# A two-layer hybrid decoder on one core: gate and up of two feature blocks by seven half-width products in place of eight

## The chip, the core and the metric

The kernel runs on one core of one Trainium2 chip. The metric is the device time of one execution in microseconds. Everything is float32; each float32 operand of a matrix product is held as two parts, a rounded "hi" part and the remainder "lo", both of type fp32r.

## The reference, cut to what matters

Two layers, each with a feed-forward network (FFN), a mixer (attention, a state-space scan and gates) and a second FFN. The change touches the FFN alone:

```python
D_MODEL, SEQ, DEPTH, FFN_HIDDEN = 1024, 512, 2, 2816

def swiglu(h, w_up, w_down):
    gate, up = jnp.split(h @ w_up, 2, axis=-1)
    return (jax.nn.silu(gate) * up) @ w_down

for l in range(DEPTH):
    x = x + 0.5 * swiglu(rms_norm(x, ffn1_norm[l]), ffn1_w_up[l], ffn1_w_down[l])
    ...                                   # the mixer
    x = x + 0.5 * swiglu(rms_norm(x, ffn2_norm[l]), ffn2_w_up[l], ffn2_w_down[l])
```

## The kernel before, in words

Activations lie transposed: 8 tiles `x` of 128 features by 512 tokens. All weights come from one flat array, in units of 128 output features; a unit of 1024 input features is 128 x 1024 in SBUF (8 blocks of 128 x 128, 512 KB). `unit_order` lists the units in the order in which TensorE (PE) uses them, and everything else follows this list.

For each unit three steps run ahead of PE. `fetch` has SyncE (SP) issue the load into `wraw` (3 buffers). `convert` has ScalarE (ACT) round it to `whi` and VectorE (DVE) subtract, which gives `wlo` (3 buffers of each). `ahead` starts the conversion of the unit two places ahead (`LOOK`) and fetches up to four ahead (`AHEAD`). PE then multiplies with `dense`: for each of the 8 blocks `mm3` makes three matmuls, whi by hi, wlo by hi and whi by lo, with the weight block as the stationary operand and 512 tokens as the moving one. A unit of 8 blocks is 24 matmuls of 512 columns into one PSUM bank.

Side work (conversions, activations, norms) is written as generators. `tick` runs one step of each after every block of `dense`, so each engine's program is one fixed order that the generators and ticks decide. Engines run their programs in order and wait for one another by semaphores.

In the FFN the 22 feature blocks of 128 go in slices of 8, 8 and 6. In a slice each block has a gate unit and an up unit; ACT takes Silu of the gate out of PSUM (`g`), DVE multiplies by up (`a`), ACT and DVE split the result (`act`, hi and lo). Then eight down units of 8 or 6 blocks consume the slice's `act` and DVE adds them to `x`. At the start of an FFN the norm's scale is not ready, so the first blocks use unnormed `h`, and DVE scales the 8 tiles `tt`; from then on `h` is the normed pair.

Of the kernel before, what the change touches and what calls it, by code (L numbers as in the profile page):

```python
# [7 lines left out]
F32 = mybir.dt.float32  # L8
# [3 lines left out]
ALU = mybir.AluOpType  # L12
# [19 lines left out]
FB = FFN // P  # L32
SLICES = ((0, 8), (8, 16), (16, 22))
EPS = 1e-6
KCONV = 4
# [48 lines left out]


def unit_order(layer):

    def ffn(f):
        for s, (j0, j1) in enumerate(SLICES):
            for j in range(j0, j1):  # L90
                yield (layer, f, "gate", j), KB
                yield (layer, f, "up", j), KB
            for m in range(KB):
                yield (layer, f, "down", s, m), j1 - j0
# [24 lines left out]
def all_units():  # L119
    table, off = {}, 0  # L120
    for layer in range(DEPTH):
        for key, n in unit_order(layer):
            table[key] = (off, n)
            off += n * P * P
    return table, off


class Builder:
# [8 lines left out]
    def __init__(self, ctx, tc, xT, wflat, par, taps, out):  # L137
        self.tc, self.nc = tc, tc.nc
        self.ctx = ctx
        self.xT, self.wflat, self.par, self.taps, self.out = xT, wflat, par, taps, out  # L140
        self.units, _ = all_units()
        self.keys = list(self.units)
        self.pos = 0
        self.raw, self.loaded = [], []
        self.count = 0
        self.side = []
        self.xd = None

    def name(self, s):
# [33 lines left out]


    def fetch(self, i):
        off, n = self.units[self.keys[i]]
        raw = self.t(self.wraw, [P, KB * P], "wraw")
        self.nc.sync.dma_start(raw[:, :n * P], self.wflat[off:off + n * P * P].rearrange("(p f) -> p f", p=P))
        self.raw.append(raw)

    def convert(self, i):
# [52 lines left out]
    def project(self, *key, swap=False, aside=False):  # L244
# [5 lines left out]
        if swap and not normed and self.scaled_blocks >= KB // 2:  # L250
            new = []
            each = self.swapped(new)
            for _ in range(len(self.hx)):
                next(each)
            self.dense(ps, w, self.h, 0, KB, each=each)
            self.h, self.normed = new, True
        else:
            self.dense(ps, w, self.h, 0, KB)
# [11 lines left out]
    def scale_blocks(self, gain):  # L270
# [3 lines left out]
        for k in range(KB):  # L274
            self.nc.vector.scalar_tensor_tensor(self.tt[k], self.x[k], gain[:, k:k + 1], self.rs,  # L275
                                                op0=ALU.mult, op1=ALU.mult)
            self.scaled_blocks = k + 1
            yield 1

    def open_norm(self, tiles, gain):  # L280
# [166 lines left out]

    def up(self, pu, g, fp, ap, act):
        while not self.gated.pop(g.name, False):
# [3 lines left out]
        yield 1  # L453
        parts = self.pair(ap, ("act", "act"))
        yield from self.split(parts, a)
        act.append(parts)

# [6 lines left out]
    def x_final(self, m, gain):  # L464
# [4 lines left out]
        else:  # L469
            self.xg.append(self.t(self.fin, [P, SEQ], "xg", bufs=KB))  # L470
        if m == 0:
# [9 lines left out]
    def ffn(self, layer, f, gain, gain_next):  # L481
        tc = self.tc
        with tc.tile_pool(name=f"act{layer}{f}", bufs=18, reuse_waits="tile") as ap, \
                tc.tile_pool(name=f"ffn{layer}{f}", bufs=3, reuse_waits="tile") as fp, \
                tc.tile_pool(name=f"hx{layer}{f}", bufs=self.SPARE, reuse_waits="tile") as hx, \
                tc.tile_pool(name=f"tt{layer}{f}", bufs=KB, reuse_waits="tile") as tp:
            self.hx = [self.pair(hx, ("xhi", "xlo")) for _ in range(self.SPARE)]
            self.gated = {}
            self.open_norm([self.t(tp, [P, SEQ], "tt") for _ in range(KB)], gain)
            for s, (j0, j1) in enumerate(SLICES):  # L490
                act = []
                last = s == len(SLICES) - 1
                for j in range(j0, j1):
                    g = self.t(fp, [P, SEQ], "g")
# [7 lines left out]
                    self.spawn(self.up(pu, g, fp, ap, act))  # L502
                for m in range(KB):
# [405 lines left out]
    def mixer(self, layer):  # L909
# [3 lines left out]
        self.open_norm(self.x, gain)  # L913
        self.hx = []
        first = []
# [95 lines left out]
    def build(self):  # L1011
# [24 lines left out]
        for layer in range(DEPTH):  # L1036
# [3 lines left out]
            if layer < DEPTH - 1:  # L1040
                self.ffn(layer, 2, par[:, G_FFN2:G_FFN2 + KB], self.pars[layer + 1][:, G_FFN1:G_FFN1 + KB])
        with tc.tile_pool(name="fin", bufs=KB, reuse_waits="tile") as self.fin:
            self.xg = []
            self.ffn(DEPTH - 1, 2, self.pars[DEPTH - 1][:, G_FFN2:G_FFN2 + KB], None)
            self.flush()
            for m in range(KB):
                nc.vector.tensor_tensor(self.xg[m], self.xg[m], self.rs, op=ALU.mult)
                nc.sync.dma_start(self.out[m], self.xg[m])
        self.xpool.__exit__(None, None, None)
# [8 lines left out]
def lay_out(inputs):  # L1058
# [6 lines left out]
    for layer in range(DEPTH):  # L1065
# [5 lines left out]
        for key, n in unit_order(layer):  # L1071
            kind = key[1] if key[1] not in (1, 2) else key[2]
            if kind in ("gate", "up"):
                w = a[f"ffn{key[1]}_w_up"][layer]
# [76 lines left out]
```

## Time and profile before

| | |
|---|---|
| median of 3 runs | 2695.17 us (2694.84 to 2695.27) |
| the profiled execution, its own time | 2694.19 us |
| its span (first to last instruction) | 2692.4 us |
| PE busy | 2661.0 us, 99% of the span |
| DVE, ACT, GpSimd (POOL) busy | 1363.8, 1103.5, 329.6 us |
| granted TensorE clock | 0.997 of full |

The stretches 987.90 to 1076.30 and 1119.80 to 1206.90 are gate and up of the first and second slice of layer 0's second FFN. In the timelines below a row is the start in us from the span's start, the duration in us, engine, line, operation, what is written and read, the shape and the count; square brackets hold the engine's idle time ahead of it and what ended it. PEld is the loading of a stationary operand, which runs beside the matmuls. A matmul's end is modelled; starts are recorded. Rows with a count are several instructions merged, so a duration there is from the first start to the last end.

### The profile page before, as it was taken

The numbers are of one execution on the slowest core, as the hardware profiler recorded it, in microseconds if no ns is written. First come the engines' busy times: TensorE is split into PE (matmuls) and PEld (weight loads), VectorE is DVE, ScalarE is ACT, GpSimd is POOL, SyncE is SP. The second block draws the span as 40 slices with busy tenths as digits, with TensorE's granted clock in tenths as the row PEclk, the third lists the DMA queues.
The fourth block names the chain that finished last, engine by engine and source line by source line (L and its number), as shares of the span: only waits on it lengthen the run. The fifth ranks groups of instructions, "written<-read, shape, count | busy, mean of one in ns | idle before, by whom it ended". The sixth has DMA issues, their size and how long they took to land.

```text
span 2692.4 us, 31240 instructions
## 1 busy us (share of the span) xinstructions
PE 2661.0 (99%) x12264; PEld 2211.6 (82%) x12264; DVE 1363.8 (51%) x1943; ACT 1103.5 (41%) x1835; POOL 329.6 (12%) x475
## 2 busy tenths in 40 slices
PE   8999999999999999999999999999999999999998
PEld 6888888888888888888888888888888888888886
DVE  6333366565665464333563333765666745733333
ACT  5222246755554243222332222567555543422223
POOL 1000011042332010000010000112332410100001
PEclk9999999999999999999999999999999999999999
DMA  3332242233323423223233222423333243232322
GB/s 131 101 97 94 95 124 82 90 111 105 114 94 116 143 91 110 94 94 102 87 101 102 94 96 90 132 70 106 104 112 109 94 135 124 95 101 94 102 92 73
DMA packets 85828, 276.15 MB, mean 103 GB/s; under 512 B 10112, under 2 KB 10368, under 8 KB 85680
## 3 DMA queue, kind: packets, MB, share of 16 engines
q1 hardware_dynamic: 84816, 273.03, 31.2%
q8 instruction: 96, 1.57, 0.2%
q10 hardware_dynamic: 864, 1.12, 0.1%
q14 instruction: 52, 0.43, 0.1%
HBM read 261.43 MB, written 12.68 MB: 102 GB/s over the span
## 4 chain that ended last, share of the span: by engine, by line
PE 90%; DVE 6%; ACT 2%; issue 1%; DMA 0%; POOL 0%; SPq 0%; DVEq 0%; ACTq 0%
PE mm L227 28%; PE mm L229 28%; PE mm L228 27%; PE pt L577 1%; PE pa L812 1%; DVE wlo L201 1%; PE pa L650 1%; ACT whi L199 1%; DVE cv L714 1%; DVE tt L275 1%; PE pa L814 1%; PE pt L797 1%; PE pt L795 1%; DVE hlo L385 0%; PE pt L411 0%
## 5 line engine op out<-in xcount | busy, mean ns | idle before, releaser
L227 PE MATMUL mm<-hhi,whi 128*128 128x512 f32 x2148 | 859.3, 400 | 0.4 <-DVE g L430 0.4
L229 PE MATMUL mm<-hlo,whi 128*128 128x512 f32 x2148 | 839.7, 391 | 1.3 <-DVE hlo L267 1.3
L228 PE MATMUL mm<-hhi,wlo 128*128 128x512 f32 x2148 | 837.3, 390 | 0.0
L199 ACT CAST whi<-wraw 128x1024 fp32r<-128x1024 f32 (+2 forms) x472 | 473.6, 1003 | 868.3 <-PE mm L229 515.3
L201 DVE TENSOR_TENSOR wlo<-wraw,whi 128x1024 fp32r<-128x1024 f32 (+2 forms) x472 | 585.2, 1241 | 405.9 <-ACT whi L199 404.2
L229 PEld LDWEIGHTS mm<-hlo,whi 128*128 128x128 f32 x2148 | 403.6, 188 | 90.2 <-DVE hlo L267 3.4
L228 PEld LDWEIGHTS mm<-hhi,wlo 128*128 128x128 f32 x2148 | 404.5, 188 | 78.6 <-issue 1.2
L227 PEld LDWEIGHTS mm<-hhi,whi 128*128 128x128 f32 x2148 | 404.4, 188 | 78.3 <-issue 2.0
L229 PE MATMUL mm<-act,whi 128*128 128x512 f32 x704 | 273.9, 389 | 0.0
L227 PE MATMUL mm<-act,whi 128*128 128x512 f32 x704 | 273.9, 389 | 0.0
L228 PE MATMUL mm<-act,wlo 128*128 128x512 f32 x704 | 273.9, 389 | 0.0
L403 POOL TENSOR_TENSOR acc<-acc,sq 128x512 f32<-128x512 f32 x39 | 53.1, 1362 | 1548.7 <-ACT sq L396 1548.7
L460 DVE SCALAR_TENSOR_TENSOR x<-mm,x 128x512 f32<-128x512 f32 x96 | 66.2, 689 | 214.9 <-PE mm L229 214.9
L438 ACT ACTIVATE g<-mm 128x512 f32<-128x512 f32 x79 | 47.3, 598 | 293.0 <-PE mm L229 293.0
L452 DVE TENSOR_TENSOR a<-mm,g 128x512 f32<-128x512 f32 x88 | 60.8, 691 | 207.7 <-PE mm L229 203.0
L714 DVE SCALAR_TENSOR_TENSOR cv<-mm,conv,cv 128x511 f32<-128x511 f32 (+2 forms) x192 | 142.7, 744 | 25.7 <-ACT cv L711 24.0
L227 PEld LDWEIGHTS mm<-act,whi 128*128 128x128 f32 x704 | 132.2, 188 | 27.5
L229 PEld LDWEIGHTS mm<-act,whi 128*128 128x128 f32 x704 | 132.2, 188 | 27.4
L228 PEld LDWEIGHTS mm<-act,wlo 128*128 128x128 f32 x704 | 132.2, 188 | 27.4
L229 PE MATMUL mm<-xlo,whi 128*128 128x512 f32 x316 | 123.0, 389 | 0.0
L228 PE MATMUL mm<-xhi,wlo 128*128 128x512 f32 x316 | 123.0, 389 | 0.0
L227 PE MATMUL mm<-xhi,whi 128*128 128x512 f32 x316 | 122.9, 389 | 0.0
(232 smaller groups left out, 2942.5 us busy)
## 6 DMA issues: line engine op xcount, KB each, us to landing
wraw<-in_wflat_dram SPq DMA_DIRECT2D x392, 512.0 KB, 3.3
wraw<-in_wflat_dram SPq DMA_DIRECT2D x64, 384.0 KB, 3.1
cumb<-cum_d SPq DMA_DIRECT2D x16, 768.0 KB, 4.0
xd<-x SPq DMA_DIRECT2D x16, 256.0 KB, 3.8
wraw<-in_wflat_dram SPq DMA_DIRECT2D x16, 256.0 KB, 2.9
x<-xd SPq DMA_DIRECT2D x16, 256.0 KB, 4.5
gd<-gs SPq DMA_DIRECT2D x12, 256.0 KB, 2.0
gd<-gm SPq DMA_DIRECT2D x12, 256.0 KB, 2.0
```

The costliest lines, as they stand in the source:

```text
L199: nc.scalar.copy(hi[:, :n], raw[:, :n])
L201: nc.vector.tensor_tensor(lo[:, :n], raw[:, :n], hi[:, :n].bitcast(F32), op=ALU.subtract)
L227: mm(ps, a[0], b[0], start=start, stop=False, **kw)
L228: mm(ps, a[1], b[0], start=False, stop=False, **kw)
L229: mm(ps, a[0], b[1], start=False, stop=stop, **kw)
L275: self.nc.vector.scalar_tensor_tensor(self.tt[k], self.x[k], gain[:, k:k + 1], self.rs, op0=ALU.mult, op1=ALU.mult)
L403: eng.tensor_tensor(self.acc, self.acc, sq, op=ALU.add)
L438: nc.scalar.activation(g, pg, AF.Silu)
L452: self.nc.vector.tensor_tensor(a, pu, g, op=ALU.mult)
L460: self.nc.vector.scalar_tensor_tensor(x, pd, 0.5, x, op0=ALU.mult, op1=ALU.add)
L577: self.nc.tensor.transpose(pt[:, cs], src[:, cs], self.ident)
L714: nc.vector.scalar_tensor_tensor(u[:, i:], ps[:, :SEQ - i], tap[KCONV - 1 - i], u[:, i:], op0=ALU.mult, op1=ALU.add)
```

## The change: what it does

Gate and up of two feature blocks j and j+1 are taken together. Cut the input features in a lower and an upper half (4 blocks each) and the tokens in halves a and b (256 columns each). A part then holds half the input features and both feature blocks (8 blocks of 128 x 128, again 512 KB). The parts are named after the seven products: "11" and "12" are the lower and upper half of gate, "22" the upper half of up; the stored part "s1" is the lower half of up. Four are sums: s1 is that lower half plus "22", s3 is it plus "11"; for both the flat array's "s1" part is loaded by SP and the second summand added by a DMA that POOL issues (`accum_op=add`) into the same buffer. s2 = s1 + "11" and s4 = s2 + "12" are made by DVE.

`combine` makes from the normed tiles `tt` the activation differences in place, once in each FFN (16 DVE operations of 256 columns, 8 ACT casts and 8 DVE remainders of 512), as pairs `th`, `tt`.

`pair_of_blocks` runs the products in the order 11, 12, s2, s1, s3, s4, 22. Each is 2 feature blocks x 4 input blocks x 3 = 24 matmuls of 256 columns. One bank ("chain") collects 11, s2, s3 and 22 one after the other and is read between them; "12" goes to a second bank, s1 and s4 to a third. ACT copies out of PSUM (`g1`, `g2`, `c`), DVE adds (`g1`, `c`, `g2`), and `activate` makes Silu, the product with up (negated) and the split, once for each token half.

This is done for all blocks from the fifth on, from the seventh in the first FFN of layer 0 (`pairs_from`): 9 + 9 + 9 + 8 = 35 pairs. The other blocks stay as they were. A unit of a pair ticks after every second block, so four times.

```diff
+SEVEN = ("11", "12", "s2", "s1", "s3", "s4", "22")
+STORED = ("11", "12", "s1", "22")
+def pairs_from(layer, f):
+    return 6 if (layer, f) == (0, 1) else 4
...
+        for i, key in enumerate(self.keys):
+            if "pair" in key and key[-1] in ("s1", "s3"):
+                self.early.setdefault(i - (5 if key[-1] == "s1" else 4), []).append(key)
...
     def fetch(self, i):
...
+        for key in self.early.get(i, ()):
+            base = key[:-1]
+            raw = self.sums[key] = self.t(self.sx, [P, KB * P], key[-1], bufs=2)
+            self.nc.sync.dma_start(raw, self.stored(base + ("s1",)))
+            self.nc.gpsimd.dma_start(raw, self.stored(base + ("22" if key[-1] == "s1" else "11",)), accum_op=ALU.add)
...
     def convert(self, i):
...
+                raw = self.sums[key] = self.t(self.sx, [P, KB * P], "s2", bufs=1)
+                a, b = self.sums[base + ("s1",)], self.sums.pop(base + ("11",))
...
+            nc.vector.tensor_tensor(raw, a, b, op=ALU.add)
+            yield 1
...
+    def combine(self):
...
+            nc.vector.tensor_tensor(u[:, a], u[:, a], u[:, b], op=ALU.subtract)
+            nc.vector.tensor_tensor(u[:, b], v[:, b], u[:, b], op=ALU.subtract)
...
+    def pair_of_blocks(self, base, fp, two):
...
+        def product(ps, part, rhs, cols, start):
+            hi, lo = self.unit(*base, part)
+            for j in range(2):
+                for k in range(n):
+                    ks = slice((j * n + k) * P, (j * n + k + 1) * P)
+                    self.mm3(ps[:, j * half:(j + 1) * half], (hi[:, ks], lo[:, ks]),
+                             [r[:, cols] for r in rhs[k]], start and j + k == 0, k == n - 1, skip_group_check=True)
+                    if k % 2:
+                        self.tick()
...
+        product(chain, "11", lower, a, True)
+        nc.scalar.copy(g1, chain)
+        product(ps2, "12", upper, a, True)
+        nc.vector.tensor_tensor(g1, g1, ps2, op=ALU.add)
+        self.spawn(activate(g1, up1, a))
+        product(chain, "s2", diff[n:], b, False)
+        nc.scalar.copy(g2, chain)
+        product(ps3, "s1", diff[:n], a, True)
+        c = self.t(fp, [P, SEQ], "c", bufs=2)
+        nc.scalar.copy(c, ps3)
+        product(chain, "s3", diff[:n], b, False)
+        nc.vector.tensor_tensor(c, chain, c, op=ALU.add)
+        up2.append(c)
+        product(ps3, "s4", upper, b, False)
+        nc.vector.tensor_tensor(g2, g2, ps3, op=ALU.add)
+        self.spawn(activate(g2, up2, b))
+        product(chain, "22", diff[n:], a, False)
+        up1.append(chain)
```

Where instructions stand now is shown at three places, all in the second FFN of layer 0. L numbers are of the kernel that the rows belong to.

PE before, at the seam from a gate unit (`mm_9311`) to an up unit (`mm_9348`); `xhi`, `hhi` and `hlo` are normed activations:

```order
L227 MATMUL mm_9311<-hhi_8274,whi_9249 128x512
L228 MATMUL mm_9311<-hhi_8274,wlo_9250 128x512
L229 MATMUL mm_9311<-hlo_8275,whi_9249 128x512
L227 MATMUL mm_9348<-xhi_8079,whi_9285 128x512 [waits Activation_49]
L228 MATMUL mm_9348<-xhi_8079,wlo_9286 128x512 [waits DVE_49]
```

PE of the change, at the seam from product "12" (`mm_10245`) to s2, which goes on in the chain bank (`mm_10244`):

```order
L269 MATMUL mm_10245<-hhi_9094,whi_10216 128x256
L270 MATMUL mm_10245<-hhi_9094,wlo_10217 128x256
L271 MATMUL mm_10245<-hlo_9095,whi_10216 128x256
L269 MATMUL mm_10244<-th_8896,whi_10265 128x256 [waits Activation_49]
L270 MATMUL mm_10244<-th_8896,wlo_10266 128x256 [waits DVE_49]
```

The three matmuls of a block stay together and each keeps its own weight load; the columns fall from 512 to 256, and the waits for `whi` (ACT) and `wlo` (DVE) come at each product's first and second matmul.

DVE before, one whole block (a gate and an up unit):

```order
L201 TENSOR_TENSOR wlo_9320<-wraw_9242,whi_9319 128x1024 [waits DMAHW5_49]
L201 TENSOR_TENSOR wlo_9356<-wraw_9279,whi_9355 128x1024 [waits DMAHW6_49,PE_49,Activation_49]
L452 TENSOR_TENSOR a_9387<-mm_9348,g_9310 128x512 [waits PE_49]
L293 TENSOR_TENSOR act_9396<-a_9387,act_9395 128x512 [waits Activation_49]
```

DVE of the change, from the last sums of one pair (chain `mm_10244`) to the start of the next; `s_1836` is the next pair's s2, `wlo_10452` belongs to its "12", `wlo_10501` to its s2 and `wlo_10529` to its s1:

```order
L572 TENSOR_TENSOR g_10248<-g_10248,pa_10246 128x512 [waits PE_49]
L551 SCALAR_TENSOR_TENSOR a_10460<-c_10382,g_10248 128x512 [waits Activation_49]
L243 TENSOR_TENSOR wlo_10452<-wraw_10384,whi_10451 128x1024 [waits DMAHW2_49,Activation_49]
L359 TENSOR_TENSOR act_10243<-a_10460,act_10242 128x2x256 [waits Activation_49]
L237 TENSOR_TENSOR s_1836_10490<-s_1810_10284,wraw_10348 128x1024 [waits DMASW0_49]
L551 SCALAR_TENSOR_TENSOR a_10498<-mm_10244,g_10247 128x512 [waits PE_49]
L359 TENSOR_TENSOR act_10243<-a_10498,act_10242 128x2x256 [waits Activation_49]
L243 TENSOR_TENSOR wlo_10501<-s_1836_10490,whi_10500 128x1024
L243 TENSOR_TENSOR wlo_10529<-s_1810_10284,whi_10528 128x1024 [waits PE_49,Activation_49]
L561 TENSOR_TENSOR g_10482<-g_10482,mm_10480 128x512 [waits PE_49]
```

ACT of the change over the same stretch:

```order
L546 ACTIVATE g_10248<-g_10248 128x512 [waits DVE_49]
L241 CAST whi_10451<-wraw_10384 128x1024 [waits DMAHW2_49,PE_49,Activation_49]
L354 CAST act_10242<-a_10460 128x2x256 [waits DVE_49]
L241 CAST whi_10500<-s_1836_10490 128x1024 [waits DVE_49,PE_49,Activation_49]
L354 CAST act_10242<-a_10498 128x2x256 [waits DVE_49]
L559 COPY g_10482<-mm_10479 128x512 [waits PE_49]
```

Before, a block's turn on DVE is two remainders of weights, one product with up and one split. Now, at the seam of two pairs, both products with up, both splits and the sum for s2 stand ahead of the remainder of s2, and on ACT the cast for s2 stands ahead of the second split's cast.

SP of the change, the same stretch: "12" and "22" of the earlier pair (`wraw_10149`, `wraw_10316`), "11" of the next (`wraw_10348`), s1 and s3 of the pair after that, and "12" of the next pair (`wraw_10384`):

```order
L210 DMA wraw_10149<-in_wflat_dram 128x1024 [waits DMAHW0_49,DVE_49]
L210 DMA wraw_10316<-in_wflat_dram 128x1024 [waits DMAHW1_49,DVE_49]
L210 DMA wraw_10348<-in_wflat_dram 128x1024 [waits DMAHW2_49,DVE_49,Activation_49]
L217 DMA s_1840_10519<-in_wflat_dram 128x1024 [waits DMASW6_49,DVE_49]
L217 DMA s_1847_10585<-in_wflat_dram 128x1024 [waits DMASW7_49,DVE_49]
L210 DMA wraw_10384<-in_wflat_dram 128x1024 [waits DMAHW5_49,DVE_49]
```

POOL's queue holds only the two adding DMAs of each pair there, each of which waits for its load (DMAHW):

```order
L218 DMA s_1840_10519<-in_wflat_dram 128x1024 [waits DMAHW0_49,DMASW6_49,DVE_49]
L218 DMA s_1847_10585<-in_wflat_dram 128x1024 [waits DMAHW1_49,DMASW7_49,DVE_49]
```

The loads of s1 and s3 stand more than one pair ahead of their use, and "12" stands behind them.

## Rows read from the trace of the kernel before

**Rows 1.** The page: span, busy time by engine, chain that ended last.

```profile
span 2692.4 us, 31240 instructions
PE 2661.0 (99%) x12264; PEld 2211.6 (82%) x12264; DVE 1363.8 (51%) x1943; ACT 1103.5 (41%) x1835; POOL 329.6 (12%) x475
PE 90%; DVE 6%; ACT 2%; issue 1%; DMA 0%; POOL 0%; SPq 0%; DVEq 0%; ACTq 0%
```

**Rows 2.** Stretches: length; busy PE, PEld, DVE, ACT, POOL; granted clock; DMA share, GB/s.

```profile
987.90:1076.30 88.40, 88.21 (x387) 72.39 (x386) 45.29 (x55) 32.22 (x44) 6.28 (x2) 1.00 0.32 100
1119.80:1206.90 87.10, 87.10 (x386) 72.12 (x386) 29.36 (x31) 24.31 (x31) 0.00 (x0) 1.00 0.29 96
```

**Rows 3.** Timeline of ACT in slice 2 of that FFN.

```profile
1136.37 0.60 ACT L438 ACTIVATE g<-mm 128x512 f32<-128x512 f32 x1 [3.87 <-PE mm L229]
1136.86 1.04 ACT L199 CAST whi<-wraw 128x1024 fp32r<-128x1024 f32 x1
1141.85 1.05 ACT L199 CAST whi<-wraw 128x1024 fp32r<-128x1024 f32 x1 [3.95 <-issue]
1142.81 0.61 ACT L288 CAST act<-a 128x512 fp32r<-128x512 f32 x1
1147.25 0.60 ACT L438 ACTIVATE g<-mm 128x512 f32<-128x512 f32 x1 [3.83 <-PE mm L229]
```

**Rows 4.** Timelines of DVE and of PE at the end of one up unit.

```profile
1130.93 0.69 DVE L452 TENSOR_TENSOR a<-mm,g 128x512 f32<-128x512 f32 x1 [2.65 <-PE mm L229]
1132.54 0.69 DVE L293 TENSOR_TENSOR act<-a,act 128x512 fp32r<-128x512 f32 x1 [0.91 <-ACT act L288]
1133.14 1.22 DVE L201 TENSOR_TENSOR wlo<-wraw,whi 128x1024 fp32r<-128x1024 f32 x1
1137.93 1.23 DVE L201 TENSOR_TENSOR wlo<-wraw,whi 128x1024 fp32r<-128x1024 f32 x1 [3.57 <-ACT whi L199]
...
1130.50 0.39 PE L229 MATMUL mm<-hlo,whi 128*128 128x512 f32 x1
1130.73 0.39 PE L227 MATMUL mm<-xhi,whi 128*128 128x512 f32 x1
```

**Rows 5.** Timelines of PE in the attention: matmuls of 256 columns, then what follows.

```profile
411.33 0.28 PE L227 MATMUL pa<-yt,yt 128*128 128x256 f32 x1
...
411.69 0.40 PE L227 MATMUL mm<-hhi,whi 128*128 128x512 f32 x1
...
440.53 0.29 PE L227 MATMUL pt<-btok,yt 128*128 128x256 f32 x1
...
440.90 0.22 PE L227 MATMUL pt<-dec,yt 128*128 128x128 f32 x1
```

**Rows 6.** Timelines of PE: a run of short matmuls, and two of 256 columns behind short ones.

```profile
2136.10 0.49 PE L577 MATMUL pt<-ident,bT 128*128 128x128 f32 x3
2136.43 0.39 PE L795 MATMUL pt<-cT,bT 128*128 128x128 f32 x2
...
2136.98 0.78 PE L812 MATMUL pa<-xdt,dec 128*128 128x64 f32 x6
...
418.11 0.45 PE L650 MATMUL pa<-xz,ntri 128*128 128x256 f32 x2
418.40 0.39 PE L227 MATMUL mm<-hhi,whi 128*128 128x512 f32 x1
```

**Rows 7.** Groups of POOL: count, busy us, mean ns, idle before.

```profile
L403 POOL TENSOR_TENSOR acc<-acc,sq 128x512 f32<-128x512 f32 x39 | 53.1, 1362 | 1548.7 <-ACT sq L396 1548.7
L444 POOL TENSOR_TENSOR g<-g,rs 128x512 f32<-128x512 f32 x9 | 26.7, 2975 | 94.8 <-ACT g L442 94.8
```

**Rows 8.** The page: DMA queue of SP (packets, MB, share), issues (KB each, us to landing).

```profile
q1 hardware_dynamic: 84816, 273.03, 31.2%
wraw<-in_wflat_dram SPq DMA_DIRECT2D x392, 512.0 KB, 3.3
x<-xd SPq DMA_DIRECT2D x16, 256.0 KB, 4.5
```

More of the change, by code (lines that the diff above doesn't have):

```diff
@@ L90, in ffn @@
             for j in range(j0, j1):
-                yield (layer, f, "gate", j), KB
-                yield (layer, f, "up", j), KB
+                if j < pairs_from(layer, f):
+                    yield (layer, f, "gate", j), KB
+                    yield (layer, f, "up", j), KB
+                elif j % 2 == 0:
+                    for part in SEVEN:
+                        yield (layer, f, "pair", j, part), KB
             for m in range(KB):
@@ L123, in all_units @@
             table[key] = (off, n)
-            off += n * P * P
+            if "pair" not in key or key[-1] in STORED:
+                off += n * P * P
     return table, off
@@ L256, in project @@
             self.h, self.normed = new, True
+            if self.th is not None:
+                self.spawn(self.combine())
         else:
@@ L453, in up, with activate @@
         yield 1
-        parts = self.pair(ap, ("act", "act"))
         yield from self.split(parts, a)
-        act.append(parts)
+    def pair_of_blocks(self, base, fp, two):
+        nc, half, n = self.nc, SEQ // 2, KB // 2
+        assert self.normed and self.combined == n
+        a, b = slice(0, half), slice(half, SEQ)
+        lower, upper = self.h[:n], self.h[n:]
+        diff = self.diff
+        chain, ps2 = (self.t(self.pmm, [P, SEQ], "mm") for _ in range(2))
+        ps3 = self.t(self.pa, [P, SEQ], "pa")
+        def product(ps, part, rhs, cols, start):
[7 more added lines that the diff above has]
+                        self.tick()
+        def activate(g, c, cols):
+            nc.scalar.activation(g, g, AF.Silu)
+            while c is None or not c:
+                yield 1
+            yield 1
+            r = self.t(fp, [P, SEQ], "a")
+            nc.vector.scalar_tensor_tensor(r, c[0], -1.0, g, op0=ALU.mult, op1=ALU.mult)
+            yield 1
+            r = r.rearrange("p (j t) -> p j t", j=2)
+            yield from self.split([t.rearrange("p (j t) -> p j t", j=2)[:, :, cols] for t in two], r)
+        up1, up2 = [], []
+        g1, g2 = (self.t(fp, [P, SEQ], "g", bufs=4) for _ in range(2))
+        product(chain, "11", lower, a, True)
[16 more added lines that the diff above has]
+        up1.append(chain)
@@ L913, in mixer @@
         self.open_norm(self.x, gain)
-        self.hx = []
+        self.hx, self.th = [], None
         first = []
@@ L1041, in build @@
                 self.ffn(layer, 2, par[:, G_FFN2:G_FFN2 + KB], self.pars[layer + 1][:, G_FFN1:G_FFN1 + KB])
[L1042 to L1048, printed above, removed]
+        self.xg = []
+        self.ffn(DEPTH - 1, 2, self.pars[DEPTH - 1][:, G_FFN2:G_FFN2 + KB], None)
+        self.flush()
+        for m in range(KB):
+            nc.vector.tensor_tensor(self.xg[m], self.xg[m], self.rs, op=ALU.mult)
+            nc.sync.dma_start(self.out[m], self.xg[m])
         self.xpool.__exit__(None, None, None)
@@ L1072, in lay_out @@
             kind = key[1] if key[1] not in (1, 2) else key[2]
-            if kind in ("gate", "up"):
+            if kind == "pair":
+                if key[-1] not in STORED:
+                    continue
+                r0, c0 = {"11": (0, 0), "12": (DM // 2, 0), "s1": (0, FFN), "22": (DM // 2, FFN)}[key[-1]]
+                c0 += key[3] * P
+                w = a[f"ffn{key[1]}_w_up"][layer][r0:r0 + DM // 2]
+                blk = np.concatenate([w[:, c0:c0 + P], w[:, c0 + P:c0 + 2 * P]])
+            elif kind in ("gate", "up"):
                 w = a[f"ffn{key[1]}_w_up"][layer]
```

66 lines of the change are left out of this document (56 added, 10 removed).

## The prediction, made before the changed kernel was run

> **What bounds the kernel now.** I read the page first: PE is busy for 2661.0 of 2692.4 us, and the chain of work that ended last runs through PE for 90% of the span [rows 1]. Then the busy time by stretch: in a middle slice of an FFN PE fills 87.10 of 87.10 us at the full granted clock (1.00, the 2.4 GHz level), while DVE works 29.36 us, ACT 24.31 us and the DMA engines show a share of 0.29 [rows 2]. So in these stretches nothing but PE's own pace matters. That pace is read from ACT's timeline, where Silu waits for PE once per block: 1136.37 to 1147.25 is 10.88 us for a gate and an up unit, 48 matmuls, so 0.2267 us each [rows 3]. 512 columns at 2.4 GHz are 0.2133, so about 0.0133 us per matmul is spent beside the columns. Two blocks cost 96 x 0.2267 = 21.76 us. What the change is worth follows from what 168 matmuls of half the columns cost, and from whether ACT and DVE keep up with products that come nearly twice as fast.
>
> **The matmuls.** The trace has 256-column matmuls of the same type in the attention, three in a row: from 411.33 to the next matmul at 411.69 is 0.36 for three, 0.120 each, and from 440.53 to 440.90 is 0.37, 0.123 each [rows 5]. The columns plus the same fixed part give 0.1067 + 0.0133 = 0.120. A weight load for each matmul does not forbid it: three transposes of 128 columns, each with a load, start 0.11 apart (2136.10 to 2136.43), and six of 64 columns a little later end 0.78 after the first started, about 0.1 apart [rows 6]; so neither the loads nor the sequencer's issue hold a short run above 0.11. I take 0.120, the value where rows and sum agree; bounds 0.118 (rounding of 0.36 down) and 0.123. A pair is then 168 x 0.120 = 20.16 us, 1.60 less than before, and 35 pairs give 56.0 us.
>
> Here a rule of the Trainium skill differs: "TensorE: Matmul & The Clock Gate", section Back-to-back issue gap, gives columns / 2.4 + 2.5 ns. For 512 columns that is 215.8 ns where the trace has 226.7. For 256 it would be 109 ns, 18.3 us a pair and 120 us in all. The trace disagrees on both widths, and I go by the rows.
>
> **ACT and DVE.** A pair turns seven units into whi and wlo (eight before) and adds two 1024-column sums, three PSUM additions, three PSUM copies. Durations: whi 1.05, wlo 1.23 (I take the sum as the same shape, 1.23), a 512-column DVE operation 0.69, ACT's PSUM read 0.60, its cast 0.61, and Silu in SBUF taken as 0.63, an estimate from these two [rows 3, 4]. An engine starts its next operation about 0.09 before the last ends (1132.54 + 0.69 against 1133.14; 1141.85 + 1.05 against 1142.81). DVE per pair: 9 x 1.14 + 7 x 0.60 = 14.5 of 20.16 us; ACT 7 x 0.96 + 7 x 0.52 = 10.4. On the mean both fit. In order they may not, so I walk the queue of one inner pair; clock 0 is the start of its product "11", a result is readable 0.20 after the next product starts (1130.93 against 1130.73 [rows 4]), a handover between engines costs 0.04 (1136.86 + 1.04 to 1137.93 [rows 3, 4]).
> The previous pair's s4 ends: g2 += at -2.68 to -1.99; ACT's Silu -1.95 to -1.32; ACT casts "12" -1.41 to -0.36; DVE's product with up -1.28 to -0.59; wlo of "12" -0.32 to 0.91; remainder of the split 0.82 to 1.51; sum s2 1.43 to 2.66; the other half's product with up 2.57 to 3.26. ACT casts s2 2.70 to 3.75, then that half's split 3.66 to 4.27. DVE, next in order, waits for this split: remainder 4.31 to 5.00, and only then wlo of s2, 4.92 to 6.15. PE begins s2 at 5.76 and its second matmul, due at 5.88, needs that wlo and 0.12 for its load (0.11 [rows 6]): 6.31. **That is a stall of 0.43 us in each inner pair.** Walking on, DVE is level again when s4 ends (17.79 against 17.75), so the lag does not add up. The copies g1, g2 and c each have a whole product (2.88 us) as cover and end in time. With no handover cost the stall is 0.2, with 0.10 per handover 0.8. The first pair in each slice (12 of 35) follows units with lighter queues and has none: 23 x 0.43 = 9.9 us, bounds 4.6 and 18.
>
> **Slice ends.** The last split now comes from the last product. By the same walk its remainder, behind one wlo on DVE, ends 3.6 us after the pair; in a slice of 8 the down units need it at 6 x 0.68 + 0.45 = 4.5, in the four slices of 6 at 3.2: 4 x 0.45 = 1.8 us; bounds 0 and 5.
>
> **Openings.** `combine` adds at most 24 x 0.69 = 16.6 us to DVE and 8 x 0.61 to ACT per FFN, where DVE is busy 45.29 of 88.40 us [rows 2]. It lies beside at least three ordinary blocks and I cost it at 0; uncovered it would be 4 x 16.6 = 66 us, which nothing in the order suggests.
>
> **DMA.** The 31.2% of 2692.4 us for 273.03 MB [rows 8] mean 1.61 us of all engines per 512 KB. Five loads per pair are 8.0 us of 20.16. The price of an adding DMA is in no row. Below: as a load, 3.3 us. Above: the slowest rate in the rows, 256 KB in 4.5 us, so 9 us for 512 KB [rows 8]. Two at 9 us in series are 18, still inside a pair. Each add has long notice: the load for s1 is issued more than a pair ahead (when the pair two before has read that buffer, about 8 on the clock above), its sum is read at 1.43 two pairs on, some 34 us later. Most exposed is the load of "12", which stands behind those: its buffer comes free when sum s4 is made, 11.9, and its cast is due at 19.2, 7 us for a load of 3.3. I cost DMA at 0. POOL, which issues the adds, does little else there (0.00 busy in the middle slices [rows 2]).
>
> POOL is slowed beside DVE: the same 128x512 product of two tiles takes 2.98 us on the mean in the openings and 1.36 elsewhere [rows 7]. Of adding DMAs the Trainium skill says, in "SBUF — State Buffer", Who interferes with whom, that a DVE copy in a two-port mode keeps GpSimd from writing descriptors but a tensor_tensor does not. The pairs' DVE queue holds no copies, so by that rule the adds are not held up; no run here shows it yet.
>
> **Sum.** 56.0 - 9.9 - 1.8 = 44.3 us. The profiled execution took 2694.19 us, 1.8 above its span; it becomes 2649.9, and as it lay 1.0 below the median, **2651 us**. Its own bounds: 0.118 gives 11.8 more gain, 0.123 up to 15 less (a slower product leaves DVE more time), stalls and slice ends +7 and -11: 2632 to 2677.
>
> **Rivals.**
> 1. *DVE and ACT become the bound.* Were the queue's turn longer than walked (the 128x2x256 splits dearer, casts held by late loads), a pair takes 21 to 22.5 us. For it: handovers at 0.10 already give 20.95. Against it: DVE idles through 28% of a pair. 2670 to 2723.
> 2. *Weight loads show.* Two 256-column matmuls behind short ones took 0.29, 0.146 each (418.11 to 418.40 [rows 6]). If that held in a stream, a pair is 24.5 us: +2.8 x 35, 2792. It decides against the change from 21.76/168 = 0.1295 on. Against it: there the load had only short matmuls to hide behind, and rows 5 show no such thing.
> 3. *The adds come late*, slower than before. Place: sum s2 and whi of s3, which wait for them, and DVE's and ACT's whole queues behind. It costs time once two adds take longer than 20 us, and decides once they take 21.8, so 10.9 us each, over three times a load. At four times (13.2 us) a pair is 26.4: +4.6 x 35, 2857. Milder: the adds crowd the load of "12"; each us beyond its 4 us of slack costs about 1 us a pair.
> 4. *Shorter matmuls.* The fixed part could shrink with the columns, down to the 0.11 of a load [rows 6]. Then the walk of DVE and ACT, about 20.1 us a pair, is the bound: 35 x 1.66 - 1.8 = 56, 2639; were the handovers free as well, 19.8 and 2628. For it: nothing in the rows; against it: rows 5. The rule of the Trainium skill's page "TensorE: Matmul & The Clock Gate" cited above would end here too.
> 5. *A matmul costs the same whatever its columns*: 168 x 0.2267 = 38.1, 3266. Rows 5 speak plainly against it.
>
> **Chances.** A measurement here tells 0.2% (5.4 us) from no change. Forecast 0.63; rival 1 0.11 (of this 0.06 faster, 0.02 same, 0.03 slower); rival 2 0.05; rival 3 0.10 (0.02 faster, 0.01 same, 0.07 slower); rival 4 0.10; rival 5 0.01. Faster: 0.63 + 0.06 + 0.02 + 0.10 = 0.81; same 0.03; slower 0.16. The range takes in the forecast, rival 4 and rival 1 as far as no change: 2626 to 2700.
>
> **What the profile would show.** Right: 256-column matmuls 0.120 apart within a product; PE's only idle time in a pair before the second matmul of s2, released by DVE's wlo, some 0.4 us, absent in a slice's first pair; copies out of PSUM never the releaser; sums released by DVE, not by a DMA. Wrong: matmuls above 0.13 apart (2); PE waiting for ACT's whi or for g and c sums at several products (1); DVE's s2 sum or ACT's s3 cast released by the adding DMA, or the load of "12" landing after 19 on the clock (3).

## The result, and the profile after

The changed kernel takes 2701.6 us (median; 2695.5 to 2703.2), the kernel before in the same comparison 2694.8 (2694.0 to 2695.9): ratio 1.0023, interval 1.0013 to 1.0032. It is slower by some 6 to 7 us, about the 0.2% that can be told here (the interval begins below that), where 2651 was forecast; the median lies outside the range of 2626 to 2700. The profiled execution took 2703.2 us, 1.7 above its span.

From the page of the changed kernel: the span, busy times, the chain that ended last, the two DMA queues (packets, MB, share of 16 engines), and the issues (KB each, us to landing):

```profile
span 2701.5 us, 37394 instructions
PE 2627.1 (97%) x14784; PEld 2291.7 (85%) x14784; DVE 1678.8 (62%) x2319; ACT 1284.8 (48%) x2077; POOL 392.5 (15%) x545
PE 69%; DVE 14%; DMA 7%; ACT 5%; issue 3%; POOL 0%; ACTq 0%; SPq 0%; DVEq 0%
...
q1 hardware_dynamic: 89856, 291.38, 34.8%
q0 software_dynamic: 10080, 36.70, 7.3%
...
wraw<-in_wflat_dram SPq DMA_DIRECT2D x357, 512.0 KB, 3.7
s<-in_wflat_dram POOLq DMA_DIRECT2D x70, 512.0 KB, 9.1
```

Against [rows 1] PE's share of the chain falls from 90% to 69%, and DMA, with 0% before, has 7%: loads now decide when PE may go on. PE's busy time fell by only 34 us, where 35 pairs of 1.60 less would give 56. In part that is the granted clock, which was not always full, as the next view shows; in part it is the view itself, since busy runs to a matmul's modelled end and so takes in the first part of each wait behind it. The next view gives one FFN, the second of layer 0, by stage (length; busy PE, PEld, DVE, ACT, POOL; granted clock; DMA share, GB/s): eight down units, four pairs, eight down units.

```profile
1076.30:1123.80 47.50, 45.70 (x194) 37.02 (x193) 17.67 (x19) 10.35 (x11) 0.00 (x0) 0.96 0.33 102
1123.80:1209.30 85.50, 83.28 (x673) 82.37 (x673) 58.39 (x61) 41.20 (x53) 6.90 (x8) 0.98 0.63 165
1209.30:1257.50 48.20, 45.78 (x194) 37.06 (x193) 17.67 (x19) 10.51 (x11) 0.00 (x0) 0.96 0.34 102
```

Four pairs take 85.50 where the forecast's terms give 80.64 + 3 x 0.43 = 81.9, and eight blocks before took 87.10 [rows 2]. The surprise is the down stage, whose matmuls the change does not touch: 47.50 and 48.20 for 192 matmuls that at 0.2267 take 43.5. What PE waits for (us in all, times, longest), and last the page's row of the matmuls that multiply `th` by `wlo` (count, busy us, mean ns, idle before):

```profile
PE mm L270 <- DVE wlo L243: 22.6, 31, 1.8
PE mm L269 <- ACT act L354: 9.9, 8, 2.3
PE mm L271 <- DVE act L359: 4.9, 8, 0.6
...
PE mm L269 <- ACT g L559: 3.4, 6, 0.9
...
L270 PE MATMUL mm<-th,wlo 128*128 128x256 f32 x840 | 241.5, 287 | 14.6 <-DVE wlo L243 14.6
```

Of the first row, 14.6 us in 23 waits lie at the second matmul of s2 (the row of `th`): the wait that the prediction names. The other 8.0 us are eight waits in the openings, up to the first pair. The view counts only idle time behind a modelled end; from start to start in PE's timeline the 23 waits cost 21.9 us, over twice the 9.9 predicted. The second and third rows are the first down unit's wait for the last split of the slice, eight times. Of the 23 inner pairs ten take 20.57 to 20.77 us, about the walk's 20.59, and 13 take 21.19 to 24.17. The longest, followed back in the chain (start, us, what), in the pair whose "11" starts at 1144.00 and the one behind it:

```profile
1154.66 1.23 DVE s L237
1155.90 8.97 DMA wraw<-in_wflat_dram
...
1165.25 1.06 ACT whi L241
1166.33 1.23 DVE wlo L243
1167.56 0.60 DVE act L359
1168.16 1.15 DVE s L237
...
1169.40 0.55 ACT whi L241
...
1171.61 1.23 DVE wlo L243
...
1172.88 0.58 PE mm L270
1173.46 0.21 PE mm L271
```

The load of "12" starts when sum s4 has freed its buffer, at 11.9 us on the prediction's clock, as walked. It lands 8.97 later, at 20.9, where its cast was due at 19.2. Behind that cast, in order, stand the split's cast and the cast of s2 on ACT, and wlo, remainder and sum s2 on DVE. PE's second matmul of s2 starts at 1172.88; the walk has it 6.31 behind the start of its pair (1164.58), at 1170.89. Half of these 2.0 us come from the first matmul of s2, which waits for the copy `g1` out of PSUM, as that copy stands on ACT behind the same casts. PE's timeline:

```profile
1171.51 0.38 PE L269 MATMUL mm<-th,whi 128*128 128x256 f32 x1 [0.88 <-ACT g L559]
```

And the matmuls behind the two waits, of 0.88 and 0.99 us, are 0.21 apart, not 0.12: from 1173.20 to 1175.20 the granted clock is 0.50, its lower level of 1.2 GHz. What lies beside that load, in the timelines of SP and POOL (start, us to issue) and in a window (columns as above):

```profile
1151.31 3.79 SPq L217 DMA_DIRECT2D s<-in_wflat_dram  x2
...
1155.41 0.86 POOL L218 DMA_DIRECT2D s<-in_wflat_dram  x1 [16.56 <-DMA s<-in_wflat_dram]
1158.85 0.86 POOL L218 DMA_DIRECT2D s<-in_wflat_dram  x1 [2.58 <-DMA s<-in_wflat_dram]
```

```profile
1158.50:1164.90 6.40, 6.40 (x56) 6.40 (x55) 4.32 (x5) 1.68 (x2) 0.86 (x1) 1.00 0.98 214
```

Two loads for s1 and s3, their two adds and the load of "12" are issued within 7.5 us, and then all 16 DMA engines are 0.98 busy for 6.4 us. On the mean of the span they are not short of time at all (34.8 + 7.3%).

### The profile page after: what moved, and what is told of

Same layout as the page of the kernel before. It is cut to its first block, busy times and chain, and to the rows that moved or that the text cites. A ratio compares the mean times of both kernels' runs of the same rounds, so it can differ in the third digit from the quotient of the medians.

```text
span 2701.5 us, 37394 instructions
## 1 busy us (share of the span) xinstructions
PE 2627.1 (97%) x14784; PEld 2291.7 (85%) x14784; DVE 1678.8 (62%) x2319; ACT 1284.8 (48%) x2077; POOL 392.5 (15%) x545
## 3 DMA queue, kind: packets, MB, share of 16 engines
q1 hardware_dynamic: 89856, 291.38, 34.8%
q0 software_dynamic: 10080, 36.70, 7.3%
## 4 chain that ended last, share of the span: by engine, by line
PE 69%; DVE 14%; DMA 7%; ACT 5%; issue 3%; POOL 0%; ACTq 0%; SPq 0%; DVEq 0%
PE mm L270 19%; PE mm L271 19%; PE mm L269 19%; DMA wraw<-in_wflat_dram 7%; DVE wlo L243 5%; ACT whi L241 3%; PE pa L270 2%; PE pa L271 2%; PE pa L269 2%; DVE s L237 1%; PE pt L709 1%; PE pa L944 1%; DVE act L359 1%; PE pa L782 1%; DVE cv L846 1%
## 5 line engine op out<-in xcount | busy, mean ns | idle before, releaser
L269 PE MATMUL mm<-hhi,whi 128*128 128x512 f32 (+1 forms) x1728 | 651.5, 377 | 0.8 <-DVE g L496 0.8
L271 PE MATMUL mm<-hlo,whi 128*128 128x512 f32 (+1 forms) x1728 | 631.7, 366 | 1.3 <-DVE hlo L311 1.2
L270 PE MATMUL mm<-hhi,wlo 128*128 128x512 f32 (+1 forms) x1728 | 629.8, 364 | 0.0
L270 PE MATMUL mm<-th,wlo 128*128 128x256 f32 x840 | 241.5, 287 | 14.6 <-DVE wlo L243 14.6
L269 PE MATMUL mm<-th,whi 128*128 128x256 f32 x840 | 240.1, 286 | 3.5 <-ACT g L559 3.4
L243 DVE TENSOR_TENSOR wlo<-s,whi 128x1024 fp32r<-128x1024 f32 x140 | 169.3, 1223 | 113.3 <-ACT whi L241 113.3
L271 PE MATMUL mm<-tt,whi 128*128 128x256 f32 x840 | 239.0, 285 | 0.0
L241 ACT CAST whi<-s 128x1024 fp32r<-128x1024 f32 x140 | 146.2, 1044 | 172.3 <-DVE s L237 171.1
L270 PEld LDWEIGHTS mm<-th,wlo 128*128 128x128 f32 x840 | 162.6, 194 | 19.2 <-DVE wlo L243 19.2
L269 PEld LDWEIGHTS mm<-th,whi 128*128 128x128 f32 x840 | 162.5, 193 | 5.5 <-ACT g L559 5.3
```

Source lines behind the costliest of these rows:

```text
L241: nc.scalar.copy(hi[:, :n], raw[:, :n])
L243: nc.vector.tensor_tensor(lo[:, :n], raw[:, :n], hi[:, :n].bitcast(F32), op=ALU.subtract)
L269: mm(ps, a[0], b[0], start=start, stop=False, **kw)
L270: mm(ps, a[1], b[0], start=False, stop=False, **kw)
L271: mm(ps, a[0], b[1], start=False, stop=stop, **kw)
```

## The experiments

"Run 3" below is experiment 3, and so on. Three theories stood at the start. **A**: the adds take so much of the DMA engines that plain loads beside them land late, a cast on ACT is late, and PE waits. **B**: the loads are late because they stand behind the loads of s1 and s3 on SP, whatever the adds do. **C**: ACT's and DVE's order alone, as walked, only longer.

**1. The adds left out.** The sums s1 and s3 then lack one summand.

```
-            self.nc.gpsimd.dma_start(raw, ..., accum_op=ALU.add)
```

> The adding DMAs are left out, so s1 and s3 are the stored lower half of up alone (the sums are missing from the output); everything else, the SP queue's order too, stays. Theory A (the adds, 9.1 us each, crowd the plain loads, a late load holds ACT's cast, and what stands behind that cast stalls PE): the stalls beyond 0.43 us at s2 and those in the down units go away, a pair takes 20.6 us, the down units of 8 blocks 43.5 us a slice, in all about 2652 us (2645 to 2660). Theory B (the loads come late because they stand behind those of s1 and s3 on SP, whatever the adds): the loads of 12 still land late, 2680 to 2700. Theory C (the order of ACT and DVE alone makes the stalls): no change, about 2700.

Measured: 2659.6 us, ratio to before 0.9871 [0.9854, 0.9887].

**2. Plain loads in the adds' place**, same queue, same bytes; the sums again lack a summand.

```
-            self.nc.gpsimd.dma_start(raw, ..., accum_op=ALU.add)
+            self.nc.gpsimd.dma_start(raw, ...)
```

> POOL issues a plain load in place of each adding DMA: the same bytes from the same place into the same buffer at the same time, without the addition (the sums are missing from the output). Theory A in its strict form (it is the addition that is dear: 327 ns a packet against 159): near the kernel without adds, 2650 to 2665 us, and this transfer lands in 4 to 6 us. If it is one transfer too many in the same burst, whatever its kind: 2685 to 2700 us. Theory C: about 2700.

Measured: 2665.1 us, 0.9892 [0.9878, 0.9907]. From its page, the queue (packets, MB, share) and the issues:

```profile
q0 software_dynamic: 10080, 36.70, 4.0%
...
s<-in_wflat_dram POOLq DMA_DIRECT2D x70, 512.0 KB, 5.7
```

The same 10080 packets took 7.3% of the engines' time as adds and 4.0% as loads, 1.8 times as much, and their landing falls from 9.1 to 5.7 us. The bytes, the queue and SP's order are the same in both, so B is refuted, and C with it: 36.6 us hang on the packets being adds. Beside plain loads the load of "12" is stretched too, to 5.07 us (1145.18 to 1150.25), but lands in time, at 17.0 on the clock.

**3. The load of "22" in a buffer of its own**, s3 in one buffer instead of two, adds as in the change.

```
+            if key[-1] == "22":
+                raw = self.t(self.sx, [P, KB * P], "22", bufs=1)
...
-            raw = self.sums[key] = self.t(self.sx, [P, KB * P], key[-1], bufs=2)
+            raw = self.sums[key] = self.t(self.sx, [P, KB * P], key[-1], bufs=2 if key[-1] == "s1" else 1)
```

> Adds kept; part 22 gets a buffer of its own and s3 one buffer in place of two, so that the load of 12 takes the buffer that 11 left and is free some 9 us earlier in the pair. The output is the whole one. Theory A: the load of 12 lands before its cast is due, the stall at s2 is 0.43 us in every inner pair and that at the start of s2 for the copy g goes; the stalls at k=6 of the down units stay unless their loads move as well: 2670 to 2690 us, 2655 if they do. Theory C: about 2700.

Measured: 2660.7 us, 0.9875 [0.9860, 0.9890], with every add still there: less than the 2670 to 2690 expected, as the down units lost their waits as well (43.50 a stage in its windows). But not because "12" came earlier. Its timelines of SP and POOL, in the pair that starts at 1133.17:

```profile
1140.48 3.79 SPq L220 DMA_DIRECT2D s<-in_wflat_dram  x2
1145.07 0.33 SPq L213 DMA_DIRECT2D wraw<-in_wflat_dram  x1
...
1148.11 1.75 POOL L221 DMA_DIRECT2D s<-in_wflat_dram  x2 [19.54 <-DMA s<-in_wflat_dram]
```

"12" is issued at 11.9 on the clock again. What moved is the first add: with one buffer for s3 the add into s3 stands first on POOL and the one into s1 behind it, and they are issued 3.0 and 3.6 us after "12" (14.9 on the clock and later). In the changed kernel the one into s1 comes first, 0.5 before "12", and the one into s3 2.95 after it.

**4. The two sums on GpSimd**, from plain loads (s3 in one buffer): a 128x1024 addition each.

```
-            self.nc.gpsimd.dma_start(raw, ..., accum_op=ALU.add)
+            b = self.raw[-1]
+            if key[-1] == "s1":
+                b = self.t(self.sx, [P, KB * P], "b", bufs=1)
+                self.nc.sync.dma_start(b, self.stored(base + ("22",)))
+            self.nc.gpsimd.tensor_tensor(raw, raw, b, op=ALU.add)
```

> The two adding DMAs are replaced by GpSimd additions of 128x1024 in SBUF (for s1 the second summand is loaded a second time, plainly; s3 has one buffer). The output is the whole one. Theory A: the loads land in 3 to 5 us again and the stalls fall to 0.43 us at s2: 2650 to 2660 us, if GpSimd's additions do not slow DVE. If they do (two of some 2.7 us or more in a 20.6 us pair, beside DVE operations that read two tiles in SBUF): DVE's remainders grow beyond 1.23 us and the pair with them, 2670 to 2720 us. Theory C: about 2700.

Measured: 2729.6 us, 1.0140 [1.0115, 1.0166], above even the 2670 to 2720 expected for a slowed DVE. Groups by form, of POOL and DVE (count, busy us, mean ns):

```profile
L222 POOL TENSOR_TENSOR s<-s,b 128x1024 f32<-128x1024 f32 x35 | 113.2, 3234 | 0.0
...
L247 DVE TENSOR_TENSOR wlo<-wraw,whi 128x1024 fp32r<-128x1024 f32 x357 | 517.2, 1450 | 109.9 <-ACT whi L245 109.3 <-PE pa L786 0.4
L555 DVE SCALAR_TENSOR_TENSOR a<-c,g 128x512 f32<-128x512 f32 x35 | 35.1, 1002 | 24.4 <-ACT g L550 24.4
L573 DVE TENSOR_TENSOR c<-mm,c 128x512 f32<-128x512 f32 x35 | 24.0, 684 | 0.9
```

No load is crowded here, but each addition takes GpSimd 2.8 to 3.2 us, and DVE's work beside it is slower: wlo 1450 ns on the mean (1285 in run 3), the product of c and g 1002 (692). The addition that reads PSUM, c, stays at 684. By overlap in the trace, 20 of these 35 ran wholly beside a GpSimd addition, in 685 ns on the mean, and 14 apart from any, in 684; wlo took 1886 ns beside and 1221 apart. PE's wait for wlo is 43.0 us in its view of waits. The Trainium skill says so, "SBUF — State Buffer", Who interferes with whom: a DVE instruction with two SBUF inputs contends with a GpSimd instruction that reads SBUF, and one with at most one SBUF input, outside the two-port modes, does not. These rows agree, on both sides of the rule.

**5. The add into s1 issued behind the add into s3**, nothing else: buffers, loads and SP's order as in the change. This asks whether run 3 won by the adds' moment or by its buffers.

```
-            self.nc.gpsimd.dma_start(raw, ..., accum_op=ALU.add)
+            if key[-1] == "s3":
+                for part, other in (("s3", "11"), ("s1", "22")):
+                    self.nc.gpsimd.dma_start(self.sums[base + (part,)], self.stored(base + (other,)), accum_op=ALU.add)
```

> The changed kernel with one move: the add into s1 is issued behind the add into s3, some 3 us later; buffers, loads and their order on SP stay. Theory A (the adds' packets fall on the load of "12", which is issued 0.5 us after the first add, and stretch it from 3.6 to 9 us): first packets come when that load is nearly over, so about 2661 us, as in the run with "22" in a buffer of its own. Rival E (that run gained by its buffers, not by when the adds run): no change, 2700 us.

Measured: 2664.9 us, 0.9887 [0.9873, 0.9902]. Its timelines of SP and POOL, and windows over the load of "12" and over the four pairs and the eight down units of the FFN shown above:

```profile
1144.60 11.69 SPq L210 DMA_DIRECT2D wraw<-in_wflat_dram  x3
1147.59 1.73 POOL L220 DMA_DIRECT2D s<-in_wflat_dram  x2 [19.45 <-DMA s<-in_wflat_dram]
```

```profile
1144.60:1148.90 4.30, 4.30 (x38) 4.30 (x37) 2.95 (x3) 3.54 (x4) 1.31 (x2) 1.00 0.70 235
1112.50:1194.40 81.90, 81.41 (x673) 80.76 (x673) 58.56 (x62) 42.20 (x55) 6.91 (x8) 1.00 0.66 171
1194.40:1238.30 43.90, 43.84 (x194) 35.98 (x193) 17.34 (x19) 9.11 (x10) 0.00 (x0) 1.00 0.37 114
```

The load lands at 1148.90, 4.30 after its issue, in a window of 0.70 busy. Four pairs take 81.90 us, the forecast's 81.9, and the down units 43.90. The add into s3 stays 3 us behind "12"; the one into s1 moves from 0.5 before it to 3.5 behind. That one issue, moved by 4 us, gives back 36.8 us with all adds and buffers in place: theory A, and rival E is refuted. What decides is when an add runs, not that it runs.

**6. The remainders of a pair's two splits one tick later**, on run 3, in pairs that another pair follows: wlo of s2 then stands ahead of the second one on DVE, and the first keeps its place ahead of the sum s2.

```
-            yield from self.split([...], r)
+            parts = [...]
+            nc.scalar.copy(parts[0], r)
+            yield 1 if base[-1] + 2 in (8, 16, 22) else 2
+            nc.vector.tensor_tensor(parts[1], r, parts[0].bitcast(F32), op=ALU.subtract)
```

> The run with "22" in a buffer of its own (2660.7 us), and in pairs that another pair follows the remainder of the second half's split one tick later, so that wlo of s2 stands ahead of it on DVE. Theory C (the walk of ACT and DVE: wlo of s2 waits behind a remainder that waits for ACT, 0.42 us in each of 23 inner pairs): 9.7 us faster, 2651 us. Rival F (PE is held by the total of DVE's queue, so the lag shows at the next product): unchanged, 2660 us.

Measured: 2651.3 us, 0.9840 [0.9825, 0.9855], the fastest of the runs that make the whole result. DVE's timeline at s2 in run 3 and then in this run, and the window of this run's four pairs:

```profile
1137.49 0.69 DVE L362 TENSOR_TENSOR act<-a,act 128x512 fp32r<-128x512 f32 x1 [1.11 <-ACT act L357]
1138.10 2.35 DVE L246 TENSOR_TENSOR wlo<-s,whi 128x1024 fp32r<-128x1024 f32 x2
```

```profile
1135.06 1.23 DVE L246 TENSOR_TENSOR wlo<-s,whi 128x1024 fp32r<-128x1024 f32 x1 [0.59 <-ACT whi L244]
1136.20 0.68 DVE L560 TENSOR_TENSOR act<-a,act 128x512 fp32r<-128x512 f32 x1
```

```profile
1111.10:1191.70 80.60, 80.60 (x673) 80.59 (x672) 58.80 (x62) 42.16 (x55) 7.00 (x8) 1.00 0.67 173
```

In run 3 DVE waits 1.11 us for ACT with wlo queued behind; here wlo takes that time, and PE fills 80.60 of 80.60 us, four pairs at 20.15. Rival F, a lag that only moves on, is refuted.

**7. `combine` left out**, on run 3; the pairs multiply plain blocks of h, so sums and differences of h are missing.

```
+        self.diff, self.combined = self.h, KB // 2
+        return
...
```

> The run with "22" in a buffer of its own (2660.7 us), with combine left out: the pairs multiply the plain blocks of h instead of their sums and differences, so the sums of h and their splits are not computed. Theory G (combine's DVE work is not hidden in the openings: 2 us at the first pair in three FFNs and about 1 us in the blocks before it in four): about 12 us faster, 2649 us. Rival H (these waits come from the first pair's own sums and casts): 2660 us.

Measured: 2649.0 us, 0.9831 [0.9816, 0.9845], 11.7 below run 3. Windows over the ordinary blocks and over the first two pairs of the same FFN, first run 3, then this run:

```profile
979.70:1025.20 45.50, 45.09 (x195) 36.27 (x195) 39.30 (x60) 22.87 (x34) 9.14 (x5) 1.00 0.57 162
1025.20:1069.50 44.30, 42.35 (x338) 41.86 (x337) 31.96 (x34) 23.18 (x31) 3.48 (x4) 0.96 0.57 149
```

```profile
978.20:1023.10 44.90, 44.72 (x195) 36.31 (x194) 30.30 (x39) 19.80 (x28) 8.80 (x5) 1.00 0.58 165
1023.10:1063.80 40.70, 40.54 (x337) 40.32 (x336) 29.04 (x31) 21.49 (x28) 3.49 (x4) 1.00 0.62 162
```

With `combine`, DVE is busy 39.30 of 45.50 us and is still behind when the first pair begins; 3.6 us of that pair and 0.6 of the blocks go with it (1.4 of them matmuls at the lower clock after a wait of 1.9 us). This is the dearest of the three openings: the other two first pairs behind four blocks take 22.19 us in run 3, 2.0 above a pair that waits for nothing.

**8. Six ordinary blocks ahead of the first pair in all FFNs**, on run 6.

```
-    return 6 if (layer, f) == (0, 1) else 4
+    return 6
```

> The run before last (own buffer for "22", remainder one tick later), and the first pair of an FFN after six ordinary blocks in all four FFNs, not in one: three pairs fewer, combine beside two more blocks. Theory G: 3 x 1.6 us lost, 3 x 3 us given back, so 4 us faster than that run, about 2647 us. Rival H: 4.8 us slower than that run, about 2656 us.

Measured: 2653.7 us, 0.9850 [0.9833, 0.9866], 2.4 slower than run 6, between theory G and rival H. The first pair then waits for nothing (20.10 us in its window), but the ordinary blocks take 69.20, where 288 x 0.2267 is 65.3 and the kernel before lost 1.3 there (88.40 less 87.10 [rows 2]): `combine` costs 2.6 us with two more blocks beside it, too.

**9. Two of combine's four subtractions on GpSimd**, on run 6.

```
-            nc.vector.tensor_tensor(u[:, a], u[:, a], u[:, b], op=ALU.subtract)
-            nc.vector.tensor_tensor(u[:, b], v[:, b], u[:, b], op=ALU.subtract)
+            nc.gpsimd.tensor_tensor(u[:, a], u[:, a], u[:, b], op=ALU.subtract)
+            nc.gpsimd.tensor_tensor(u[:, b], v[:, b], u[:, b], op=ALU.subtract)
```

> The run at 2651.3 us (own buffer for "22", remainder one tick later), and the first two subtractions of combine on GpSimd instead of DVE: 8 operations of 128x256 per FFN, some 3.5 us of DVE. Theory G (DVE's total work before the first pair holds PE by 3.1 us in each of three FFNs): up to 9 us faster, 2642 to 2647 us. Rival I (GpSimd's operations take longer and slow DVE's beside them, as in the run with sums on GpSimd, and DVE waits for them in order): 2651 to 2665 us.

Measured: 2656.5 us, 0.9861 [0.9846, 0.9876], 5.3 slower than run 6: rival I. DVE's timeline beside POOL's, in the ordinary blocks:

```profile
1012.42 0.95 DVE L337 SCALAR_TENSOR_TENSOR tt<-tt,tt 128x256 f32<-128x256 f32 x1 [1.73 <-POOL tt L335]
...
1019.25 0.41 DVE L337 SCALAR_TENSOR_TENSOR tt<-tt,tt 128x256 f32<-128x256 f32 x1
...
1011.65 0.74 POOL L335 TENSOR_TENSOR tt<-tt,tt 128x256 f32<-128x256 f32 x1
```

DVE waits for GpSimd, and its operation takes 0.95 us beside GpSimd's and 0.41 alone.

**10. All four weight sums on DVE**, from plain loads (s3 in one buffer).

```
+            if key[-1] == "s3":
+                nc.vector.tensor_tensor(raw, raw, self.sums.pop(key[:-1] + ("11",)), op=ALU.add)
...
+                nc.vector.tensor_tensor(a, a, self.sums.pop(base + ("b",)), op=ALU.add)
```

> The changed kernel with all four weight sums made by DVE from plain loads, no adding DMA: two more 128x1024 additions per pair (1.22 us each), the sum s1 just ahead of s2 in DVE's queue. Theory A: no load of "12" is late; what is left is DVE's order, whose stall at the second matmul of s2 grows by the 1.14 us of one more addition: 0.42 + 1.14 in each of 23 inner pairs, 36 us, and one addition more at the first matmul of a slice's first pairs: about 2686 us. Rival: the two additions fit beside PE, as DVE is busy 62% of the span: 2660 us. If adds are not what costs: 2700 us or more.

Measured: 2700.5 us, 1.0025 [1.0014, 1.0036], slower than the 2686 expected and in the place that the expectation gave to "adds are not what costs". PE's timeline shows other waits than those of the changed kernel: the second matmul of s2 waits 1.36 us in all inner pairs (the 0.42 of run 3 plus 0.94, where 1.14 was expected), s4's wlo is now late as well, 9.6 us over 34 pairs, and s2's first matmul, 7.5 us over the 23 inner pairs. So the time of the changed kernel itself tells nothing of its cause: with no add at all one can arrive at the same 2701.

## Why the prediction was wrong

**The matmuls** were right. In PE's timeline the first pair of the first FFN, which waits for nothing, takes 20.15 us, 168 at 0.120, and run 6 keeps this pace through all inner pairs. 56.0 us were there to be had. With a weight load for every matmul, rivals 2, 4 and 5 did not appear, and 120 ns stand against the 109 ns that follow from the Trainium skill's "TensorE: Matmul & The Clock Gate", Back-to-back issue gap; the section gives that formula for a matmul by itself.

**DMA cost 0: this is the step that failed.** The prediction priced an add by its own landing, at most 9 us (it is 9.1 on the median), and found that harmless, which is true: in DVE's waits no sum waits for its add. It then took the load of "12" at 3.3 us, with 4 us of slack, beside a pair's other transfers. The loads of s1 and s3 are issued when DVE has read those buffers, "12" when sum s4 has, and the three come within 5 us, so two adds of nearly double-priced packets run over that load. The prediction's own clock held the clash: the load of s1 at about 8, landed 3.3 later, its add from 11.3 on for up to 9 us, and the load of "12" at 11.9. Runs 2 and 5 show it from two sides. It is the milder form of rival 3, which had a chance and a price per us, but no size of its own in the sum; rival 1 names the same chain from ACT's side ("casts held by late loads"). The price of about 1 us per us was right: where the trace has the landing, "12" 0.5 us late costs its pair 0.6 over run 3's 20.57, and 1.3 late 1.4. Two pairs with 1.7 late cost 3.6 and 3.3, as some of their matmuls run at half clock as well. Of the places, the prediction had only one: the second matmul of s2 waits at most 1.36 us (11 of 23 pairs), and the rest falls on the first, behind the copy `g1`, which the walk had found covered. So the sign "copies out of PSUM never the releaser" failed too.

**Slice ends**, put at 1.8 us with bounds 0 and 5, cost most: the eight down stages behind slices of 8 take 371.0 us in PE's timeline against 8 x 43.5 = 348.2. The walk had put the last split's remainder behind one wlo on DVE. It left out that ACT's cast for a down unit, in order ahead of the split's cast, may itself be held by a late load. ACT's and PE's timelines at such an end:

```profile
1213.80 1.04 ACT L241 CAST whi<-wraw 128x1024 fp32r<-128x1024 f32 x1 [2.27 <-DMA wraw<-in_wflat_dram]
1214.75 0.61 ACT L354 CAST act<-a 128x512 fp32r<-128x512 f32 x1
...
1215.42 0.50 PE L269 MATMUL mm<-act,whi 128*128 128x512 f32 x1 [1.81 <-ACT act L354]
1216.76 0.50 PE L271 MATMUL mm<-act,whi 128*128 128x512 f32 x1 [0.61 <-DVE act L359]
```

Where loads are in time, in runs 3 and 6, the slices of 8 end with none, as walked, and those of 6 with 0.1 us instead of 0.45.

**The walk of ACT and DVE** was right in place and size: 9.7 us in 23 inner pairs in run 3 (9.9 predicted), none in first pairs, and gone when the order is turned (run 6). In the changed kernel itself the same place costs 21.9, since late casts enter that queue.

**Openings at 0** was wrong by 12 us. Run 7 gives 11.7 for `combine`, mainly DVE being some 2 us behind at the second matmul of the first "11" in three FFNs. The work was counted rightly (16.6 us at most) but compared with the mean of 45.29 in 88.40 us, not with what lies between the swap and the first pair.

The account, in us of span: forecast 2648.1; pairs beyond their 715.5 +27.5, of which 19.9 in the inner pairs and 7.6 in three first pairs, behind `combine`; down stages of 8 +22.8; openings and all else +4.5; slices of 6 -1.5; together 2701.4 against 2701.5. Some 7 of these are matmuls at the lower clock level, behind waits (in PE's timeline 44 of 256 columns at +93 ns, 14 of 512 at +200). Without the crowding, run 5, the forecast's own mechanism gives 2664.9 rather than 2651; the rest is `combine` (11.7) and what is left of the slice ends. Of its signs for "wrong", the third came true: the load of "12" landing after 19. That run 6 ends at the forecast's 2651 is chance: it has neither the stalls (9.9) nor the slice ends (1.8) that the forecast counted, and has `combine`, which the forecast left out. That DVE's tensor_tensor does not hold off descriptor writing, the rule cited from the Trainium skill, was not measured by itself; run 2's plain loads, issued by POOL beside the same DVE work, landed in 5.7 us. And [rows 7] do not show that POOL is slowed beside DVE as such: they set an addition (1.36) against a product (2.98), and in the trace most of these additions ran beside DVE too. Nothing in the sum rests on it.

## What to carry to other kernels

Price a transfer not only by when its own result is due but by what it does to the most exposed load beside it: walk the issue times of all queues on one clock and look for bursts, since a mean DMA share of 42% hid 6.4 us at 0.98. When a late load feeds an in-order engine, list everything queued behind its consumer up to the next place where the faster engine waits; stages that the change does not touch can pay as much as those it does. An issue moved by 4 us, or one operation's place in a queue, can be worth as much as the change was to bring: the two together (run 6), with the same adds, end at 2651.3 against 2694.5 before.

## What the runs showed of the hardware

An adding DMA's packets of the same size took 1.8 times as long as plain ones in the same queue (7.3% against 4.0% of the engines for 36.70 MB); a 512 KB add landed 9.1 us after its issue, a plain load from the same queue 5.7, and one from SP 3.7.

GpSimd's additions slowed DVE only where DVE read both inputs from SBUF (692 to 1002 ns; 0.41 to 0.95 us), and not where one came from PSUM (686 and 684 ns).

Some waits of one to two us were followed by matmuls at half the clock (0.21 apart for 256 columns; a granted clock of 0.50 from 1173.20 to 1175.20 in the changed kernel); the kernel before, whose PE does not pause in its middle slices, has none there [rows 2].
